# The opening of a decoder step in finer pieces, and raw weights held in four parts

## The chip, the cores and the metric

The kernel runs on one core of a Trainium2 chip. The metric is the device time of one execution in microseconds (us), the median of several runs. The engines have short names: PE is TensorE (matmuls; PEld its weight loads), DVE VectorE, ACT ScalarE, POOL GpSimd, SP SyncE, which issues most of the DMAs here.

## The reference

One layer of a hybrid decoder, for a prompt of 256 tokens and 8 single-token samples, which go through the projections together as 264 columns. All of it is float32.

```
proj = rms_norm(x, g_mix) @ w_in               # 2048 -> 1024+2*256+2048+3072+32
q, k, v, z, xbc, dt = split(proj)
x = x + concat(swa(q, k, v), ssd(z, xbc, dt)) @ w_out
x = x + cross_attend(rms_norm(x, g_cross), memory) @ w_co
x = x + (silu(gate) * val) @ w_down            # gate, val = conv(rms_norm(x, g_ffn) @ w_up)
```

`swa` is attention over a window of 128 with learned sinks, `ssd` a Mamba-2 mixer; the outputs hold the new caches and states too. Nearly all of the arithmetic is in the products with w_in, w_out, w_up and w_down.

## The kernel before

Activations stand with features on the 128 partitions and tokens along the columns. x is 16 blocks (`KB`) of 128 features by 264 tokens, in four tiles `xT[0..3]` of four blocks.

**Three products for one.** To multiply float32 numbers at the fast rate, each operand is split into a rounded part and a rest, both of type float32r: hi = round(x) on ScalarE (L87, L98), lo = x - hi on VectorE (L88, L99). `mm3` (L101) then issues three matmuls: hi.hi, hi.lo, lo.hi. For x the split also multiplies by the norm's gain, from the first 16 columns of `par`; the norm's own factor `r0` is applied when results leave PSUM.

**Weights** come as units of 2048 columns (1 MB): eight k-blocks of 256 output columns. `weights` (L69) takes a raw tile `wraw` of 2048 columns (two such buffers), loads it by one DMA on SP's queue, and makes two halves of 1024 columns, `whi` and `wlo` (four buffers each). A raw buffer is free again when both halves have been subtracted. `proj` runs the matmuls of two units for 256 output columns, and this goes on through the whole layer with other stages between: attention, the SSD scan, cross-attention and the convolutions. There is a priority for weights, and the order of instructions on the engines is set by the framework's planner, which simulates a timeline.

**The opening** (L149 to L191) is in a block in which SP, PE, ACT and DVE keep the order of the text. The memset of `acc0` feeds 14 warm-up matmuls (L156). SP issues `par`, the first quarter of x, the first unit of w_in in two pieces, the weights of dt (`w_dt`, 512 columns), three more quarters of x, and the second unit. `split_x(c)` splits four blocks. PE then runs, for the first 256 output columns, `first_k(k)` (six matmuls a block, into the two banks `first`) and for dt `dt_k(k)` (three a block, into `dt_ps`): 16 blocks each, so 96 and 48 matmuls. Behind the block come the squares of x (`sw`, L252 to L259) whose sum gives `r0`, which frees the banks of `first` and of dt.

ScalarE has to load a table before its first activation; before, that stands ahead of the first split of x.

Of the kernel before, what the change touches and what calls it, by code (L numbers as in the profile page):

```python
# [7 lines left out]
F32 = mybir.dt.float32  # L8
F32R = mybir.dt.float32r
AF = mybir.ActivationFunctionType  # L10
ALU = mybir.AluOpType
# [36 lines left out]
def hybrid_decoder_step_kernel(ctx: ExitStack, tc: tile.TileContext, I, O):  # L48
# [11 lines left out]
    def psum(tag):  # L60
        return ps.tile([128, 512], F32, tag=tag, name=tag, bufs=banks[tag])
# [7 lines left out]
    def weights(src, n=2048, into=None, step=2048):  # L69

        out = []
        with tc.high_priority():
            raw = wpool.tile([128, 2048], F32, tag="wraw", name="wraw", bufs=2)[:, :n]
            if step < n:
                for o in range(0, n, step):
                    nc.sync.dma_start(out=raw[:, o:o + step], in_=src[:, o:o + step])
            else:
                nc.sync.dma_start(out=raw, in_=src)
            for o in range(0, n, NPART):
                w = min(NPART, n - o)  # L80
                if into:
                    hi, lo = into
                else:
                    hi = wpool.tile([128, w], F32R, tag="whi", name="whi", bufs=WBUFS)
                    lo = wpool.tile([128, w], F32R, tag="wlo", name="wlo", bufs=WBUFS)
                x = raw[:, o:o + w]
                S.copy(out=hi, in_=x)  # L87
                V.tensor_tensor(out=lo, in0=x, in1=hi.bitcast(F32), op=ALU.subtract)  # L88
                out.append((hi, lo))
        return out  # L90
# [50 lines left out]
    def split_x(c):  # L141
        for k in range(4 * c, 4 * c + 4):
            split(A[k // 8][0][:, k % 8, :], A[k // 8][1][:, k % 8, :], xT[c][:, k % 4, :], par[:, k:k + 1])

    def load_x(c):
        nc.sync.dma_start(out=xT[c], in_=I["xT"][:, 4 * c:4 * c + 4, :])


    acc0 = small.tile([128, T], F32, tag="acc", bufs=1, name="acc0")  # L149
    dt_ps = psum("mm")  # L150
    first = [psum("t") for _ in range(2)]
    warm = psum("x")
    with tc.manual_schedule(engines={mybir.EngineType.SP, mybir.EngineType.PE, mybir.EngineType.Activation, mybir.EngineType.DVE}):
        V.memset(acc0, 0.0)
        for _ in range(14):
            PE.matmul(warm[:, :T], acc0[:, 0:128], acc0, start=True, stop=True)  # L156
        nc.sync.dma_start(out=par[:, 0:16], in_=I["par"][:, 0:16])
        load_x(0)
        split_x(0)
        pre = weights(w_in[0], step=1024)  # L160
        dthi, dtlo = (w.rearrange("p (k c) -> p k c", c=32) for w in weights(I["w_dt"], 512, (w2[:, 0:512], w2[:, 512:1024]))[0])
        for c in range(1, 4):
            load_x(c)
            split_x(c)
        pre = pre + weights(w_in[1])
# [4 lines left out]
        def first_k(k):  # L170
            wh, wl = (w.rearrange("p (k c) -> p k c", c=256) for w in pre[k // 4])
            for m in range(2):
                mm3(first[m][:, :T], wh[:, k % 4, m * 128:(m + 1) * 128], wl[:, k % 4, m * 128:(m + 1) * 128],
                    A[k // 8][0][:, k % 8, :], A[k // 8][1][:, k % 8, :], k == 0, k == KB - 1)
# [6 lines left out]
        for k in range(4):  # L181
            first_k(k)
        for k in range(4):
            dt_k(k)
        for k in range(4, 8):
            dt_k(k)
            first_k(k)
        for k in range(8, KB):
            dt_k(k)
        for k in range(8, KB):  # L190
            first_k(k)  # L191
# [61 lines left out]
    for i in range(2):  # L253
        for j in range(2):
            S.activation(out=sw[i][:, 4 * j:4 * j + 4, :], in_=xT[2 * i + j], func=AF.Square)
        V.tensor_tensor(out=sw[i][:, 0:4, :], in0=sw[i][:, 0:4, :], in1=sw[i][:, 4:8, :], op=ALU.add)
# [1034 lines left out]
```

## Time and profile before

| | |
|---|---|
| median of 3 runs | 1441.08 us (1439.83 to 1441.81) |
| the profiled execution | 1435.89 us, its span 1434.1 us |
| PE / DVE / ACT / POOL busy | 1413.7 / 1071.7 / 774.9 / 149.9 us |
| DMA | 304.64 MB, mean 212 GB/s over the span |
| granted clock, mean | 0.995 |

Times in the views count from the span's start. "xT<-in_xT_dram" is a write of the tile xT from the DRAM input xT; "<-" behind an idle time names what ended it; SPq is SP's queue of DMA issues. A row of the chain of waits has its start, its length and what ran or was waited for. Matmuls are pipelined: a row's own length is longer than the distance to the next start, and a stretch's count divided by its length gives the pace. "PEclk" or the number ahead of the DMA share is the granted clock of TensorE.

### The profile page before, as it was taken

How to read it: one execution, taken by the hardware profiler on the slowest of the kernel's cores; microseconds unless marked ns; L12 is line 12 of the kernel's file. 1: busy time of each engine (PE TensorE's matmuls, PEld its weight loads, DVE VectorE, ACT ScalarE, POOL GpSimd, SP SyncE). 2: the span in 40 equal slices, each digit the busy share in tenths (PEclk: the TensorE clock that was granted, in tenths of full speed). 3: DMA queues.
4: the chain of work that ended last, by engine and by line, in shares of the span. 5: the costliest groups of instructions: out<-in, count | busy, mean ns of one | idle time of the engine just before them, and what ended most of it. 6: DMA issues, size and time to landing. Idle time of an engine off the chain costs nothing.

```text
span 1434.1 us, 28668 instructions
## 1 busy us (share of the span) xinstructions
PE 1413.7 (99%) x11481; PEld 1387.9 (97%) x11481; DVE 1071.7 (75%) x2066; ACT 774.9 (54%) x1297; POOL 149.9 (10%) x330
## 2 busy tenths in 40 slices
PE   9999999999999999989999999999999999999999
PEld 8998899999999999978999999999999999999999
DVE  6849869999986777779677775677577757665664
ACT  6547754556645455656555653565355535543532
POOL 0000001111104212015001010001000100010000
PEclk9999999999999999999999999999999999999999
DMA  6853347776667556856566766566566655555554
GB/s 253 293 203 118 127 155 228 250 251 229 209 229 275 195 177 216 342 223 241 207 221 221 239 222 213 200 229 235 183 213 220 224 176 191 196 189 187 180 189 149
DMA packets 59365, 304.64 MB, mean 212 GB/s; under 512 B 8864, under 2 KB 13920, under 8 KB 29664
## 3 DMA queue, kind: packets, MB, share of 16 engines
q1 hardware_dynamic: 53728, 283.94, 56.5%
q0 software_dynamic: 5504, 18.88, 3.6%
q8 instruction: 90, 1.47, 0.4%
q14 instruction: 43, 0.35, 0.1%
HBM read 287.06 MB, written 16.28 MB: 212 GB/s over the span
## 4 chain that ended last, share of the span: by engine, by line
PE 89%; DVE 4%; DMA 4%; ACT 2%; POOL 1%; issue 1%; SPq 0%; ACTq 0%; DVEq 0%; POOLq 0%
PE mm L103 19%; PE mm L102 19%; PE mm L104 19%; PE t L102 9%; PE t L104 9%; PE t L103 9%; DVE wlo L88 1%; DMA wraw<-in_w_out_dram 1%; DMA vt<-in_mvT_dram 1%; ACT whi L87 1%; PE s L439 1%; DVE kt L924 1%; PE t L208 1%; DVE vt L953 1%; DMA wraw<-in_w_in_dram 1%
## 5 line engine op out<-in xcount | busy, mean ns | idle before, releaser
L87 ACT CAST whi<-wraw 128x1024 fp32r<-128x1024 f32 x448 | 466.1, 1049 | 531.7 <-PE mm L103 284.7
L88 DVE TENSOR_TENSOR wlo<-wraw,whi 128x1024 fp32r<-128x1024 f32 x448 | 552.4, 1238 | 229.4 <-ACT whi L87 227.6
L102 PE MATMUL t<-x2h,whi 128*128 128x264 f32 x704 | 200.7, 285 | 3.0 <-ACT whi L87 3.0
L103 PE MATMUL t<-x2l,whi 128*128 128x264 f32 x704 | 200.1, 284 | 0.0
L102 PE MATMUL mm<-x2h,whi 128*128 128x264 f32 x704 | 199.9, 284 | 0.2 <-DVE res L1023 0.2
L104 PE MATMUL t<-x2h,wlo 128*128 128x264 f32 x704 | 199.9, 284 | 0.0
L103 PE MATMUL mm<-x2l,whi 128*128 128x264 f32 x704 | 199.8, 284 | 0.0
L104 PE MATMUL mm<-x2h,wlo 128*128 128x264 f32 x704 | 199.4, 283 | 0.0
L103 PE MATMUL mm<-hl,whi 128*128 128x264 f32 x704 | 198.8, 283 | 0.0
L104 PE MATMUL mm<-hh,wlo 128*128 128x264 f32 x704 | 198.4, 283 | 0.0
L102 PE MATMUL mm<-hh,whi 128*128 128x264 f32 x704 | 197.5, 284 | 0.0
L102 PE MATMUL mm<-xh,whi 128*128 128x264 f32 x608 | 176.6, 292 | 0.7 <-ACT whi L87 0.7
L103 PE MATMUL mm<-xl,whi 128*128 128x264 f32 x608 | 175.0, 289 | 0.0
L104 PE MATMUL mm<-xh,wlo 128*128 128x264 f32 x608 | 174.6, 291 | 0.0
L102 PEld LDWEIGHTS t<-x2h,whi 128*128 128x128 f32 x704 | 133.1, 189 | 3.2 <-ACT whi L87 3.2
L103 PEld LDWEIGHTS t<-x2l,whi 128*128 128x128 f32 x704 | 133.2, 189 | 0.0
L102 PEld LDWEIGHTS mm<-x2h,whi 128*128 128x128 f32 x704 | 132.4, 188 | 0.4 <-ACT sq L220 0.4
L104 PEld LDWEIGHTS t<-x2h,wlo 128*128 128x128 f32 x704 | 132.4, 188 | 0.3 <-DVE wlo L88 0.3
L103 PEld LDWEIGHTS mm<-x2l,whi 128*128 128x128 f32 x704 | 132.6, 188 | 0.0
L103 PEld LDWEIGHTS mm<-hl,whi 128*128 128x128 f32 x704 | 132.5, 188 | 0.0
L104 PEld LDWEIGHTS mm<-x2h,wlo 128*128 128x128 f32 x704 | 132.1, 188 | 0.0
L104 PEld LDWEIGHTS mm<-hh,wlo 128*128 128x128 f32 x704 | 132.0, 188 | 0.0
(418 smaller groups left out, 3042.6 us busy)
## 6 DMA issues: line engine op xcount, KB each, us to landing
wraw<-in_w_up_dram SPq DMA_DIRECT2D x88, 1024.0 KB, 4.9
wraw<-in_w_in_dram SPq DMA_DIRECT2D x51, 1024.0 KB, 5.4
wraw<-in_w_dn_dram SPq DMA_DIRECT2D x44, 1024.0 KB, 4.9
wraw<-in_w_out_dram SPq DMA_DIRECT2D x24, 1024.0 KB, 4.9
h<-in_h_dram POOLq DMA_DIRECT2D x32, 256.0 KB, 5.0
hn<-in_h_dram SPq DMA_DIRECT2D x16, 512.0 KB, 6.7
out_state_s_dram<-hn POOLq DMA_DIRECT2D x16, 512.0 KB, 3.4
pb<-dram_p SPq DMA_DIRECT2D x4, 1028.0 KB, 10.0
```

Of the source, the lines that this page charges most:

```text
L87: S.copy(out=hi, in_=x)
L88: V.tensor_tensor(out=lo, in0=x, in1=hi.bitcast(F32), op=ALU.subtract)
L102: PE.matmul(out, wh, xh, start=start, stop=False)
L103: PE.matmul(out, wh, xl, start=False, stop=False)
L104: PE.matmul(out, wl, xh, start=False, stop=stop)
L208: PE.transpose(out, in_, cst[0:k, C_ID:C_ID + k])
L439: PE.matmul(s3, qT[:, j, c * 128:c * 128 + 128], kbd[:, pp, :, 0:nk], start=True, stop=True)
L924: V.scalar_tensor_tensor(out=x, in0=x, scalar=1.0, in1=qb[:, 2 * b + m, :], op0=ALU.mult, op1=ALU.mult, accum_out=lg[:, kb, row:row + 1])
L953: V.scalar_tensor_tensor(out=vt[:, b, m, :], in0=vt[:, b, m, :], scalar=1.0, in1=pbs[row // 8][:, row % 8, 0:256], op0=ALU.mult, op1=ALU.m ...
```

## The change

- The raw weights are held in four buffers of 1024 columns (`raw_part`), and every load is one of 1024 columns (512 KB, or 256 KB for dt) with its own buffer, in the whole kernel.
- ScalarE runs a Copy on one column (`table`) early, and issues two DMAs itself: par and the first 512 columns of the first unit.
- In the opening x is loaded in eight pieces of two blocks, the first unit in four pieces of 512 columns, in turn. The splits go block by block in the same turn; the first weight piece is rounded on VectorE.
- 8 warm-up matmuls instead of 14.
- `first_k` runs the three products of a block for both output halves in turn (hi.hi twice, hi.lo twice, lo.hi twice), and the order of blocks is: first 0 to 7, dt 0 to 7, first 8 to 15, dt 8 to 15.
- The squares of x are ordered behind the last split.

```diff
@@ -66,24 +66,22 @@
 
     NPART, WBUFS = 1024, 4
 
-    def weights(src, n=2048, into=None, step=2048):
+    def raw_part(n=NPART):
+        return wpool.tile([128, n], F32, tag="wraw", name="wraw", bufs=4)
+
+    def weights(src, n=2048, into=None):
 
         out = []
         with tc.high_priority():
-            raw = wpool.tile([128, 2048], F32, tag="wraw", name="wraw", bufs=2)[:, :n]
-            if step < n:
-                for o in range(0, n, step):
-                    nc.sync.dma_start(out=raw[:, o:o + step], in_=src[:, o:o + step])
-            else:
-                nc.sync.dma_start(out=raw, in_=src)
             for o in range(0, n, NPART):
                 w = min(NPART, n - o)
+                x = raw_part(w)
+                nc.sync.dma_start(out=x, in_=src[:, o:o + w])
                 if into:
                     hi, lo = into
                 else:
                     hi = wpool.tile([128, w], F32R, tag="whi", name="whi", bufs=WBUFS)
                     lo = wpool.tile([128, w], F32R, tag="wlo", name="wlo", bufs=WBUFS)
-                x = raw[:, o:o + w]
                 S.copy(out=hi, in_=x)
                 V.tensor_tensor(out=lo, in0=x, in1=hi.bitcast(F32), op=ALU.subtract)
                 out.append((hi, lo))
@@ -138,57 +136,109 @@
     for h in range(2):
         A.append((T3(apool, 8, F32R, "A", f"xh{h}", 4), T3(apool, 8, F32R, "A", f"xl{h}", 4)))
 
-    def split_x(c):
-        for k in range(4 * c, 4 * c + 4):
-            split(A[k // 8][0][:, k % 8, :], A[k // 8][1][:, k % 8, :], xT[c][:, k % 4, :], par[:, k:k + 1])
-
-    def load_x(c):
-        nc.sync.dma_start(out=xT[c], in_=I["xT"][:, 4 * c:4 * c + 4, :])
+    def load_x(j):
+
+        nc.sync.dma_start(out=xT[j // 2][:, 2 * (j % 2):2 * (j % 2) + 2, :], in_=I["xT"][:, 2 * j:2 * j + 2, :])
+
+    def x_of(k):
+        return xT[k // 4][:, k % 4, :], par[:, k:k + 1]
+
+    def x_hi(k):
+        x, g = x_of(k)
+        return S.activation(out=A[k // 8][0][:, k % 8, :], in_=x, func=AF.Copy, scale=g)
+
+    def x_lo(k):
+        x, g = x_of(k)
+        return V.scalar_tensor_tensor(out=A[k // 8][1][:, k % 8, :], in0=x, scalar=g, in1=A[k // 8][0][:, k % 8, :].bitcast(F32),
+                                      op0=ALU.mult, op1=ALU.subtract)
+
+
+    wraw0 = [raw_part() for _ in range(2)]
+    pre = [tuple(wpool.tile([128, NPART], F32R, tag=t, name=t, bufs=WBUFS) for t in ("whi", "wlo")) for _ in range(2)]
+
+    def w_piece(q):
+        cs = slice(512 * (q % 2), 512 * (q % 2) + 512)
+        return wraw0[q // 2][:, cs], pre[q // 2][0][:, cs], pre[q // 2][1][:, cs]
+
+    def w_load(q, on):
+        on.dma_start(out=w_piece(q)[0], in_=w_in[0][:, 512 * q:512 * q + 512])
+
+    def w_hi(q):
+        raw, hi, _ = w_piece(q)
+        S.copy(out=hi, in_=raw)
+
+    def w_lo(q):
+        raw, hi, lo = w_piece(q)
+        V.tensor_tensor(out=lo, in0=raw, in1=hi.bitcast(F32), op=ALU.subtract)
 
 
     acc0 = small.tile([128, T], F32, tag="acc", bufs=1, name="acc0")
+    table = small.tile([128, 1], F32, tag="r", bufs=2, name="table")
     dt_ps = psum("mm")
     first = [psum("t") for _ in range(2)]
     warm = psum("x")
     with tc.manual_schedule(engines={mybir.EngineType.SP, mybir.EngineType.PE, mybir.EngineType.Activation, mybir.EngineType.DVE}):
         V.memset(acc0, 0.0)
-        for _ in range(14):
+        load_x(0)
+        S.dma_start(out=par[:, 0:16], in_=I["par"][:, 0:16])
+        w_load(0, S)
+
+        S.activation(out=table, in_=acc0[:, 0:1], func=AF.Copy)
+        for _ in range(8):
             PE.matmul(warm[:, :T], acc0[:, 0:128], acc0, start=True, stop=True)
-        nc.sync.dma_start(out=par[:, 0:16], in_=I["par"][:, 0:16])
-        load_x(0)
-        split_x(0)
-        pre = weights(w_in[0], step=1024)
-        dthi, dtlo = (w.rearrange("p (k c) -> p k c", c=32) for w in weights(I["w_dt"], 512, (w2[:, 0:512], w2[:, 512:1024]))[0])
-        for c in range(1, 4):
-            load_x(c)
-            split_x(c)
-        pre = pre + weights(w_in[1])
+        for q in range(1, 4):
+            w_load(q, nc.sync)
+            load_x(q)
+        x_hi(0)
+        raw, hi, _ = w_piece(0)
+        V.tensor_copy(out=hi, in_=raw)
+        x_hi(1)
+        x_lo(0)
+        w_lo(0)
+        x_lo(1)
+        for q in range(1, 4):
+            w_hi(q)
+            w_lo(q)
+            for k in (2 * q, 2 * q + 1):
+                x_hi(k)
+                x_lo(k)
+        dthi, dtlo = (w.rearrange("p (k c) -> p k c", c=32) for w in weights(I["w_dt"].rearrange("p k c -> p (k c)"), 512, (w2[:, 0:512], w2[:, 512:1024]))[0])
+        for h in range(2):
+            raw = raw_part()
+            nc.sync.dma_start(out=raw, in_=w_in[1][:, 1024 * h:1024 * h + 1024])
+            hi, lo = (wpool.tile([128, NPART], F32R, tag=t, name=t, bufs=WBUFS) for t in ("whi", "wlo"))
+            for j in (4 + 2 * h, 5 + 2 * h):
+                load_x(j)
+            S.copy(out=hi, in_=raw)
+            V.tensor_tensor(out=lo, in0=raw, in1=hi.bitcast(F32), op=ALU.subtract)
+            pre.append((hi, lo))
+            for k in range(8 + 4 * h, 12 + 4 * h):
+                xsplit = x_hi(k), x_lo(k)
         nc.sync.dma_start(out=cst, in_=I["cst"])
         nc.sync.dma_start(out=par[:, 16:], in_=I["par"][:, 16:])
         nc.sync.dma_start(out=hcol, in_=I["hcol"])
 
         def first_k(k):
-            wh, wl = (w.rearrange("p (k c) -> p k c", c=256) for w in pre[k // 4])
-            for m in range(2):
-                mm3(first[m][:, :T], wh[:, k % 4, m * 128:(m + 1) * 128], wl[:, k % 4, m * 128:(m + 1) * 128],
-                    A[k // 8][0][:, k % 8, :], A[k // 8][1][:, k % 8, :], k == 0, k == KB - 1)
+            wh, wl = (w.rearrange("p (k c) -> p k c", c=256)[:, k % 4, :] for w in pre[k // 4])
+            xh, xl = (a[:, k % 8, :] for a in A[k // 8])
+
+            for i, (w, x) in enumerate(((wh, xh), (wh, xl), (wl, xh))):
+                for m in range(2):
+                    PE.matmul(first[m][:, :T], w[:, m * 128:(m + 1) * 128], x, start=k + i == 0, stop=k == KB - 1 and i == 2)
 
         def dt_k(k):
             mm3(dt_ps[0:32, :T], dthi[:, k, :], dtlo[:, k, :], A[k // 8][0][:, k % 8, :], A[k // 8][1][:, k % 8, :],
                 k == 0, k == KB - 1)
 
 
-        for k in range(4):
+        for k in range(8):
             first_k(k)
-        for k in range(4):
+        for k in range(8):
             dt_k(k)
-        for k in range(4, 8):
-            dt_k(k)
+        for k in range(8, KB):
             first_k(k)
         for k in range(8, KB):
             dt_k(k)
-        for k in range(8, KB):
-            first_k(k)
 
     def pc(name, i=0, n=1):
         o = _PC[name][0]
@@ -250,10 +300,11 @@
 
 
     sw = [T3(apool, 8, tag="B", name=f"sw{i}", bufs=4) for i in range(2)]
-    for i in range(2):
-        for j in range(2):
-            S.activation(out=sw[i][:, 4 * j:4 * j + 4, :], in_=xT[2 * i + j], func=AF.Square)
-        V.tensor_tensor(out=sw[i][:, 0:4, :], in0=sw[i][:, 0:4, :], in1=sw[i][:, 4:8, :], op=ALU.add)
+    with tc.issue_after(xsplit[0].ins), tc.issue_after(xsplit[1].ins):
+        for i in range(2):
+            for j in range(2):
+                S.activation(out=sw[i][:, 4 * j:4 * j + 4, :], in_=xT[2 * i + j], func=AF.Square)
+            V.tensor_tensor(out=sw[i][:, 0:4, :], in0=sw[i][:, 0:4, :], in1=sw[i][:, 4:8, :], op=ALU.add)
     V.tensor_tensor(out=sw[0][:, 0:4, :], in0=sw[0][:, 0:4, :], in1=sw[1][:, 0:4, :], op=ALU.add)
     V.tensor_tensor(out=sw[0][:, 0:2, :], in0=sw[0][:, 0:2, :], in1=sw[0][:, 2:4, :], op=ALU.add)
     V.tensor_tensor(out=acc0, in0=sw[0][:, 0, :], in1=sw[0][:, 1, :], op=ALU.add)
```

## The prediction

> **What bounds the kernel now.** I read the totals of the page first, then TensorE's list of waits, then the opening along the chain of waits and the timeline, then the chain round the longest later stall, and last the DMA and queue lists.
>
> The totals, and what TensorE waited for (microseconds in total, times, the longest):
>
> ```profile
> span 1434.1 us, 28668 instructions
> ...
> PE 1413.7 (99%) x11481; PEld 1387.9 (97%) x11481; DVE 1071.7 (75%) x2066; ACT 774.9 (54%) x1297; POOL 149.9 (10%) x330
> ...
> PE mm L102 <- ACT whi L87: 3.5, 2, 2.8
> ...
> PE y L853 <- ACT sq L898: 2.8, 1, 2.8
> PE t L104 <- DVE wlo L88: 1.6, 3, 0.7
> ```
>
> TensorE (PE) is the bound: 99% busy, VectorE 75%, ScalarE 54%. A change that leaves the matmuls alone can only win what PE loses: the time before its first useful matmul, and 20 us idle (1434.1 - 1413.7). The warm-up matmuls count as busy, so the opening's loss does not show in the 99%. It shows in the chain at the start (start, length, what):
>
> ```profile
> 0.74 0.39 SPq L157
> ...
> 1.19 3.98 DMA xT<-in_xT_dram
> ...
> 5.25 1.28 ACT L98
> ...
> 6.54 1.73 ACT xh L98 x4
> 8.27 0.97 ACT sw L255
> 9.25 0.94 ACT whi L87
> ...
> 10.21 1.24 DVE wlo L88
> ...
> 11.49 0.39 PE t L104
> ```
>
> x lands at 5.17. Only then does ScalarE load its table (1.28), split four blocks (1.73), take a sum-of-squares step that could wait (L255, about 1), and cast the first 1024 columns (0.94). On PE:
>
> ```profile
> 10.23 0.39 PE L102 MATMUL t<-xh,whi 128*128 128x264 f32 x1
> 10.46 0.28 PE L103 MATMUL t<-xl,whi 128*128 128x264 f32 x1
> 11.49 0.39 PE L104 MATMUL t<-xh,wlo 128*128 128x264 f32 x1 [0.75 <-DVE wlo L88]
> ```
>
> Useful work begins at 10.23 and runs on only from 11.49: 1.03 between two starts. Pace of PE in three stretches (length, busy and count, granted clock, DMA share, GB/s):
>
> ```profile
> 1.20:6.20 5.00, 5.00 (x11) 1.00 0.80 256
> 6.20:10.10 3.90, 3.90 (x18) 1.00 1.02 392
> 11.49:28.70 17.21, 17.21 (x141) 1.00 0.64 239
> ```
>
> From 11.49 to 28.70 there is a matmul every 0.122 us (17.21 / 141) and no gap: the opening's 144 matmuls (96 for the first columns, 48 for dt) are never starved again. So the opening's end is its start plus 17.6 us.
>
> **The change part by part.** *Warm-ups, 14 to 8.* Each is two instructions. Eleven of them fit into 1.20 to 6.20 (0.45 each), then 18 into 3.9 us (0.22 each). Sixteen are through at 6.2 + 5 x 0.22 = 7.3, and 7.4 with the step between the two paces. That is the earliest start of useful work.
>
> *The order of loads.* Before, SP issued par, then 528 KB of x, then weights. After, SP issues 264 KB of x first, and ScalarE's queue issues par (8 KB) and 256 KB of weights meanwhile. Data in the opening (length, PE, PEld, DVE, ACT, POOL busy; clock; DMA share; GB/s):
>
> ```profile
> 2.00:3.00 1.00, 1.00 (x4) 0.79 (x3) 0.00 (x0) 0.00 (x0) 0.00 (x0) 1.00 0.75 127
> 3.00:4.00 1.00, 1.00 (x3) 0.68 (x3) 0.00 (x0) 0.00 (x0) 0.00 (x0) 1.00 0.93 317
> 4.00:11.00 7.00, 6.75 (x25) 5.12 (x23) 2.50 (x5) 5.74 (x8) 0.00 (x0) 1.00 1.02 389
> ```
>
> About 450 KB have moved by 4.0, then 389 a us; the old par and x (536 KB) had moved by 4.2 and landed at 5.17, a lag of 1.0. The new x piece, par and weight piece together are 528 KB, and the first goes out at 0.74 instead of 1.19: moved by 4.2 - 0.45 and landed at about 4.7. Two DMA issues on ScalarE cost about 0.4 each by SP's row (0.39), beside the loads; the table's 1.28 follows and is over by about 3, also beside the loads. First useful operands: x split 0.43 (1.73 / 4), at the same time VectorE's cast of 512 columns, at most the 0.61 of ScalarE's cast below, hence 5.3. PE is not free before 7.4, so that cover is 2 us deep; if the first loads come over 2 us late, every further us costs one.
>
> *Feeding.* Costs of a half of 512 columns and of a block of x:
>
> ```profile
> 11.04 0.61 ACT L87 CAST w<-wraw 128x512 fp32r<-128x512 f32 x1
> ...
> 12.49 0.68 DVE L88 TENSOR_TENSOR w<-wraw,w 128x512 fp32r<-128x512 f32 x1
> ...
> 13.10 1.70 DVE L99 SCALAR_TENSOR_TENSOR xl<-xT,par,xh 128x264 fp32r<-128x264 f32 x4
> ```
>
> PE needs 12 x 0.122 = 1.46 us for two blocks; VectorE needs 0.68 + 2 x 0.43 = 1.54, ScalarE 0.61 + 0.86 = 1.47. VectorE's first pair (with its cast) ends at 4.7 + 0.6 + 1.54 = 6.8, the fourth at 6.8 + 3 x 1.54 = 11.4. The data for it: 2088 KB moved at 4.0 + (2088 - 450) / 389 - 0.45 = 7.8, landed 1.0 later by the lag above, plus one pair's 1.54: 10.3. PE reaches that pair at 7.4 + 3 x 1.46 = 11.8. So it is fed, by 0.4. SP's seven issues of x and weights end by 0.74 + 7 x 0.45 = 3.9. The last quarter of the second weight unit takes the first buffer again, free after 6.8 + 0.68 = 7.5, and five issues stand behind it on SP (two of x, cst, par, hcol). With dt, the unit's other half and the x between, its bytes have moved by 4.0 + (3896 - 450) / 389 - 0.45 = 12.4 and landed by 13.4; PE wants it at 7.4 + 96 x 0.122 = 19.1. The squares, which now stand behind the last splits, feed r0:
>
> ```profile
> 33.21 1.80 DVE L213 RECIPROCAL r<-r 128x264 f32<-128x264 f32 x1 [0.38 <-ACT r L212]
> ```
>
> It was there at 35.0 and wanted at 28.7 + 96 x 0.122 = 40.4, where the third pair of columns needs the dt bank: 5.4 to spare, and with the splits over earlier the squares start hardly later. All these I put at nothing, hidden by the slack named; without it each costs its lateness. The new order of the three products asks for the low weight last, which is what removes the 0.91 stall (1.03 less 0.12).
>
> *Opening's sum.* Start 10.23 to 7.4: 2.8. Stall 0.9. At most 3.7; I take 3.4, as VectorE is 0.08 slower than PE for each pair. Ends: nothing, were PE fed no faster than before, and 3.7.
>
> *Clock.* The row has the faster pace from 6.2, five us after the first warm-up. The Trainium skill (TensorE: Matmul & The Clock Gate, Part 1: The HAM clock gate) says that the array is released only by a busy window of about 3.4 us that runs freely, so the moment differs from run to run; the granted clock in these rows reads 1.00 throughout, and only the pace shows the step. By the trace's moment the opening gives 3.4; by that rule at its late end (8.0, an estimate from the page's window) it gives about 1 less.
>
> *Raw weights in quarters.* Every later load becomes two of 512 KB, each released by its own subtraction. It matters where PE waited for raw weights. The longest, in the chain round 404:
>
> ```profile
> 391.51 1.06 ACT whi L87
> ...
> 393.69 1.21 DVE wlo L88
> ...
> 394.93 7.92 DMA wraw<-in_w_out_dram
> ...
> 402.94 1.05 ACT whi L87
> ...
> 404.04 0.39 PE mm L102
> ```
>
> and the other half of the released buffer, on VectorE, with PE's count round it:
>
> ```profile
> 389.81 1.21 DVE L88 TENSOR_TENSOR wlo<-wraw,whi 128x1024 fp32r<-128x1024 f32 x1
> ...
> 400.00:404.00 4.00, 1.24 (x11) 1.00 0.85 305
> ```
>
> PE did 11 matmuls where 33 fit: about 2.8 lost (its wait row says 2.8). The first half was done with at 391.0, but the load waited for the second, to 394.93. After, it is issued 3.9 us earlier and carries half. What a half takes, issue to landing, is nearest to these:
>
> ```profile
> wraw<-in_w_up_dram SPq DMA_DIRECT2D x88, 1024.0 KB, 4.9
> ...
> res<-in_xT_dram SPq DMA_DIRECT2D x4, 528.0 KB, 3.9
> ...
> wraw<-in_w_in_dram SPq DMA_DIRECT2D x2, 512.0 KB, 5.7
> ```
>
> So 394.9 to 398.9 even at the crowded 7.92, cast by 400: no wait. I take 2.8 here, the rest (0.7 in the same row, 3.5 - 2.8, and smaller) at nothing since VectorE is late there too. Ends: a loss, priced as a rival, and 3.0 + 0.7 + 2.8 if that and the wait of L853 near 580 go too. Issues: 226 more at 0.33 to 0.4 on SP, which waits most of the time.
>
> *Against halves* speaks the Trainium skill (DMA: Bandwidth & Descriptors, Bandwidth): batch to 1 MiB for three quarters of the peak. Its fit (2.0 us plus bytes / 436 GB/s) gives 3.2 for a half and 4.4 for a whole (estimates from the page); the rows have 3.9 and 4.9, and pieces of 256 to 528 KB ran at 389 GB/s in the opening.
>
> **Sum.** 3.4 + 2.8 = 6.2. The profiled execution took 1435.89 for a span of 1434.1; it would be 1429.7. The median of the three runs is 1441.08, 5.2 above it, so the predicted median is 1434.9.
>
> **Rivals.** *Opening alone:* the rest is planned anew and the stall at 404 stays or moves. For it: VectorE, ScalarE and PE run in an order that follows from the program's plan. 1437.7.
>
> *The wait of L853 goes too.* The cast ahead of it on ScalarE waited for this load, issued behind a subtraction:
>
> ```profile
> 568.48 7.30 DMA wraw<-in_w_ck_dram
> ```
>
> 2.8 more: 1432.1. Against it: the landing of 7.30 shows a crowded queue, in which a half gains less.
>
> *The opening is fed no faster:* blocks arrive in the same FIFO, the start moves but PE then stalls, and only the 0.9 is left: 1440.2. Against it, the 389 GB/s.
>
> *The clock turns late:* sixteen instructions at 0.45 end at 8.4, 1.0 lost: 1435.9.
>
> *SP's waits (slower).* SP already waits for earlier landings before it issues weights:
>
> ```profile
> SPq L78 <- DVE wlo L88: 665.9, 132, 13.6
> SPq L78 <- DMA wraw<-in_w_in_dram: 28.7, 13, 5.1
> ...
> 583.90 12.74 DMA vt<-in_mvT_dram
> ```
>
> With twice the issues such waits come oftener, and a landing takes 12.74 near 584. A quarter held up behind one comes 12.74 - 4.9 = 7.8 late; from 3.4 on that eats the opening. 1441.1 + 7.8 - 3.4 = 1445.5. Against it: PE has up to four cast parts (11.7 us) in hand.
>
> *Halves do not overlap,* the page's rule taken to its end: 448 x 3.9 = 1747 us of loading, longer than the span: about 1750. The opening's 389 GB/s speaks against it.
>
> **How the numbers follow.** Forecast 0.34, opening alone 0.25, L853's wait too 0.10, fed no faster 0.13, clock late 0.05, SP's waits 0.08, no overlap 0.02, nothing at all 0.03. A measurement tells 0.2%, 2.9 us, from no change. Opening alone lies 0.5 past that line, so I count 0.19 of it as faster: 0.34 + 0.10 + 0.05 + 0.19 = 0.68 faster; 0.06 + 0.13 + 0.03 = 0.22 the same; 0.10 slower. The range runs from 1430.5 (L853's wait too, the 0.7, and what of the 1.6 of L104 is not the opening's 0.75) to 1440.5 (fed no faster); outside are 0.10 slower and some 0.05 below. The likeliest case alone, 1432 to 1437.
>
> **What would show it.** Right: a table load before 3 us; the first useful matmul at 7.4 to 8.4 and no gap over 0.3 behind it; the opening's last at about 25 instead of 28.7; no stall of 3 us near 400; a wraw landing near 3.9. Wrong: gaps on PE between 8 and 13 with x or weights as releaser; new rows of PE waiting for a cast that waited for a load; landings of a half near 5 in the steady stretches.

## The result, and the profile after

The changed kernel took **1425.38 us** (median of 4 runs, 1422.11 to 1426.13) against 1440.45 (1438.64 to 1441.81) for the kernel before on the same chip: a ratio of 0.9895, interval 0.9867 to 0.9924, or 15 us less. The forecast was 1434.9 with a range down to 1430.5: the sign was right, the size under half, and the time lies below the range.

The profiled execution took 1426.13, 9.8 less than the one of before (1435.89). The other 5 of the 15 lie in the executions: before's profiled one was among its quickest, after's the slowest of its four. The section on the prediction takes that up.

The totals of the page:

```profile
span 1424.3 us, 29300 instructions
...
PE 1408.7 (99%) x11469; PEld 1385.7 (97%) x11469; DVE 1067.6 (75%) x2069; ACT 774.4 (54%) x1299; POOL 142.7 (10%) x330
```

The longest rows of TensorE's list of waits (total, times, longest):

```profile
PE mm L100 <- DVE t L331: 1.9, 1, 1.9
PE y L275 <- POOL accx L271: 1.7, 1, 1.7
PE s L1049 <- ACT e L1021: 1.7, 1, 1.7
...
PE y L284 <- POOL accm L271: 1.0, 1, 1.0
```

Idle time fell only from 20.4 (1434.1 - 1413.7) to 15.6 (1424.3 - 1408.7), but busy time fell by 5 as well. Of these, 3.9 are the warm-ups, which count as busy: 9.0 of busy time stand ahead of the first useful matmul before, 5.1 after. A stretch at half clock counts as busy too, but this execution did not have less of that: between the opening's first matmuls and the end TensorE ran at half clock for 13.6 us before and for 17.1 after. The three long waits of before (2.8 to 3.0, two of them for a cast of weights, one at the attention's norm) have gone. New is the first row: the third pair of columns waits for `r0`.

**The opening.** On the timeline of the changed kernel, ScalarE's table load and then TensorE:

```profile
1.67 1.28 ACT L186 ACT_TABLE_LOAD   x1 [1.67 <-PEq L1326]
...
1.20 5.45 PE L188 MATMUL x<-acc 128*128 128x264 f32 x16 [1.20 <-DVE eps L254]
6.29 0.59 PE L227 MATMUL t<-xh,whi 128*128 128x264 f32 x2
...
36.25 0.28 PE L102 MATMUL mm<-xh,wlo 128*128 128x264 f32 x1
38.39 0.36 PE L100 MATMUL mm<-xh,whi 128*128 128x264 f32 x1 [1.86 <-DVE t L331]
```

Useful work starts at 6.29 and goes on without a gap of 0.3 to 36.25. Then 2.14 pass between two starts, with what follows it in the view by stretches (length, busy and count of PE, PEld, DVE, ACT, POOL; granted clock; DMA share; GB/s):

```profile
6.29:24.40 18.11, 18.11 (x147) 17.29 (x146) 16.12 (x33) 16.37 (x29) 0.00 (x0) 1.00 0.87 336
...
38.20:42.10 3.90, 3.71 (x18) 3.74 (x19) 3.24 (x9) 1.89 (x4) 0.00 (x0) 0.56 0.99 367
```

A granted clock of 0.56 is a stretch of 3.4 us at half clock with a little around it: 18 matmuls in 3.9 us where 32 fit, so 1.7 us lost behind a wait of 1.9.

**Where the time went.** The start of the matmul with the same number, counted from the last one, in both profiled executions (after less before; times are those of before; the order of the matmuls differs in places):

| stretch of before | after less before at its end | in the stretch | what |
|---|---|---|---|
| 0 to 36 | -4.7 | -4.7 | earlier start, no stall |
| 36 to 55 | -1.0 | +3.7 | wait for r0 (2.1), half clock (1.7) |
| 55 to 389 | -1.1 | -0.1 | 1.5 lost near 210 (a slow stretch of 6.8 for one of 3.4), won back by 389 |
| 389 to 410 | -4.3 | -3.3 | wait at 404 gone |
| 410 to 574 | -3.2 | +1.1 | new wait for the norm's sum (L284, 1.0) |
| 574 to 585 | -7.75 | -4.6 | wait of L853 gone, and its half-clock stretch |
| 585 to 675 | -5.5 | +2.2 | several small, a slow stretch of 6.8 from 622 for one of 3.4 |
| 675 to 686 | -10.4 | -4.9 | wait at 679 gone, and its half-clock stretch |
| 686 to the end | -10.4 | 0.0 | (the span ends 9.8 earlier) |

The three places by stretches, before and then after:

```profile
388.00:410.00 22.00, 19.20 (x153) 18.45 (x152) 20.32 (x40) 10.67 (x19) 1.33 (x1) 1.00 0.58 202
575.00:590.00 15.00, 12.24 (x92) 12.04 (x91) 12.82 (x72) 10.20 (x15) 0.00 (x0) 0.89 0.87 323
670.00:684.00 14.00, 11.01 (x78) 10.49 (x77) 10.70 (x14) 7.11 (x9) 2.94 (x5) 0.88 0.47 178
```

```profile
388.00:410.00 22.00, 22.00 (x180) 21.52 (x179) 20.47 (x42) 11.17 (x20) 3.34 (x2) 1.00 0.57 193
575.00:590.00 15.00, 15.00 (x128) 14.92 (x127) 12.66 (x63) 8.39 (x12) 0.00 (x0) 1.00 0.97 366
670.00:684.00 14.00, 14.00 (x118) 14.00 (x118) 11.39 (x18) 9.63 (x13) 0.68 (x5) 1.00 0.70 220
```

In the same 15 and 14 us TensorE does 36 and 40 matmuls more, and the granted clock goes from 0.89 and 0.88 to 1.00: wait and slow stretch went together there. The wait of 2.8 at 404 had no slow stretch behind it.

What held the third of them, on ScalarE's timeline before and after:

```profile
673.30 0.60 ACT L1096 ACTIVATE c<-u,par 128x256 f32<-128x256 f32 x1 [6.51 <-issue]
...
677.99 2.93 ACT L87 CAST whi<-wraw 128x1024 fp32r<-128x1024 f32 x3
```

```profile
665.08 1.05 ACT L85 CAST whi<-wraw 128x1024 fp32r<-128x1024 f32 x1 [2.00 <-DMA wraw<-in_w_up_dram]
667.82 0.60 ACT L1147 ACTIVATE c<-u,par 128x256 f32<-128x256 f32 x1 [1.70 <-DVE u L1134]
```

Before, the cast's load of 1 MB was issued at 663.44 and landed 10.8 later, at 674.2, and in ScalarE's order the cast stood behind two convolution steps (a chain through GpSimd and VectorE). After, the first quarter lands at 665 and its cast stands ahead of the convolution.

The loads themselves, a half now (KB, median us from issue to landing):

```profile
wraw<-in_w_up_dram SPq DMA_DIRECT2D x176, 512.0 KB, 3.9
wraw<-in_w_in_dram SPq DMA_DIRECT2D x102, 512.0 KB, 4.7
```

Twice as many; the half of w_up comes 1.0 sooner than the whole did (4.9).

### The profile page after: what moved, and what is told of

Same layout as the page of the kernel before. It is cut to its first block, busy times and chain, and to the rows that moved or that the text cites. A ratio compares the mean times of both kernels' runs of the same rounds, so it can differ in the third digit from the quotient of the medians.

```text
span 1424.3 us, 29300 instructions
## 1 busy us (share of the span) xinstructions
PE 1408.7 (99%) x11469; PEld 1385.7 (97%) x11469; DVE 1067.6 (75%) x2069; ACT 774.4 (54%) x1299; POOL 142.7 (10%) x330
## 4 chain that ended last, share of the span: by engine, by line
PE 91%; DVE 3%; DMA 2%; POOL 1%; ACT 1%; issue 1%; SPq 0%; ACTq 0%; POOLq 0%; DVEq 0%
PE mm L100 20%; PE mm L101 20%; PE mm L102 19%; PE t L100 9%; PE t L102 9%; PE t L101 9%; DVE wlo L86 1%; PE t L227 1%; DMA wraw<-in_w_out_dram 1%; PE s L490 1%; POOL accm L271 1%; DMA pb<-dram_p 1%; PE t L258 1%; PE t L519 1%; PE y L703 1%
## 5 line engine op out<-in xcount | busy, mean ns | idle before, releaser
L86 DVE TENSOR_TENSOR wlo<-wraw,whi 128x1024 fp32r<-128x1024 f32 x444 | 544.3, 1228 | 230.3 <-ACT whi L85 228.5
## 6 DMA issues: line engine op xcount, KB each, us to landing
pb<-dram_p SPq DMA_DIRECT2D x4, 1028.0 KB, 10.4
```

## The experiments

The theory: the gain comes from halves of a unit landing and being released by themselves, which removes long waits for weights with their half-clock stretches; the opening's own gain is mostly taken back by r0. The rivals: the opening carries the gain; the halves' size alone does it, not the ring of four; a new plan of the whole kernel removed the waits by chance.

Most edits make the planner write the order anew: with six warm-ups more, TensorE's order differs after 146 useful matmuls. So a single time within some 3 us says little of the edit; the waits in the trace say more. In three runs of parts 3 and 4 the order stayed: with the squares at high priority and with the square root's table the operations and tiles of all engines come in the order of the changed kernel, and without the early table they do but for six places on ScalarE and VectorE.

**1. The two parts alone** (one batch; before 1437.33 us).

The ring alone, in the kernel before:

```
-            raw = wpool.tile([128, 2048], F32, tag="wraw", name="wraw", bufs=2)[:, :n]
...
+                x = raw_part(w)          # [128, 1024], bufs=4
+                nc.sync.dma_start(out=x, in_=src[:, o:o + w])
```

> The kernel before with one edit: raw weights in four buffers of 1024 columns, one load each; its old opening stays. In the changed kernel the opening's gain of 4.6 us shrinks to 1.0 by 55 us, and 9.4 of the 10.4 come later. Theory Q (a quarter released by its own subtraction is loaded sooner, which removes the waits for raw weights near 404 and in front of L853 near 580): 6 to 10 us below before, and both waits gone. Theory P (every edit makes the planner put the work in another order, and the later waits move by chance): anywhere within 5 us of before, with other waits. Theory O (the opening carries the gain): within 1.5 us of before.

Measured: 1431.17 us, ratio 0.9948 (0.9929 to 0.9967). By the trace the waits near 404, 580 and 679 are gone, worth 3.3, 4.6 and 4.9; new waits (1.6 for the squares of q near 59, 1.6 for the scan near 297, 1.2 for the norm's sum near 460) and a slow stretch of 6.8 from 626 (3.4 before) take back nearly half (the span is 7.0 shorter).

The opening alone, with two raw buffers of 2048:

```
-    wraw0 = [raw_part() for _ in range(2)]
+    raw0 = wpool.tile([128, 2048], F32, tag="wraw", name="wraw", bufs=2)
+    wraw0 = [raw0[:, 0:1024], raw0[:, 1024:2048]]
```

> The changed kernel with raw weights as before: two buffers of 2048 columns, one load for a whole unit except in the opening. Theory Q: 1 to 4 us below before (the opening, less what a late r0 takes back), with the waits near 404 and in front of L853 still there. Theory P: anywhere within 5 us of before. Theory O: 10 to 15 us below before.

Measured: 1442.43 us, ratio 1.0034 (1.0015 to 1.0052): slower, where the theory had 1 to 4 us faster. Its useful work starts 4.1 earlier than before's, but then TensorE's timeline has three waits:

```profile
17.30 0.51 PE L231 MATMUL t<-xh,whi 128*128 128x264 f32 x2 [1.62 <-ACT xh L150]
18.54 0.51 PE L231 MATMUL t<-xl,whi 128*128 128x264 f32 x2 [0.74 <-DVE xl L154]
24.63 0.59 PE L102 MATMUL mm<-xh,whi 128*128 128x264 f32 x1 [3.17 <-ACT whi L87]
```

and SP's queue, of this kernel and then of the changed one, shows why:

```profile
4.21 0.53 SPq L78 DMA_DIRECT2D wraw<-in_w_dt_dram  x1
10.88 0.33 SPq L212 DMA_DIRECT2D wraw<-in_w_in_dram  x1
11.25 0.91 SPq L143 DMA_DIRECT2D xT<-in_xT_dram  x2
```

```profile
4.08 0.52 SPq L79 DMA_DIRECT2D wraw<-in_w_dt_dram  x1
5.17 0.33 SPq L208 DMA_DIRECT2D wraw<-in_w_in_dram  x1
5.54 1.27 SPq L141 DMA_DIRECT2D xT<-in_xT_dram  x2
```

With two whole buffers the second unit waits until 10.88 for a free one, and x stands behind it. With four parts it goes out at 5.17. So the opening needs the ring. The waits near 407, 583 and 682 are all there again (2.8, 1.9 and 1.8 between starts).

The two parts do not add up: the ring alone gives 6 us, the opening alone loses 5, and both together give 15. By the profiles the changed kernel's span is 2.8 below that of the ring alone (4.8 in the changed kernel's second profile, below). Of this the opening shows 0.9 (1.2) at 55, and the ring's wait near 59, which the changed kernel does not have, another 1.9. The rest, and why the medians show more (0.9948 against 0.9895), is open.

**2. Size or release.** The kernel before, every unit by two DMAs of 1024 columns into one buffer of 2048:

```
-    def weights(src, n=2048, into=None, step=2048):
+    def weights(src, n=2048, into=None, step=1024):
```

> The kernel before, where every unit is loaded by two DMAs of 1024 columns into one buffer of 2048 columns, so that the second load is sent with the first and the buffer is released whole. Theory Q: within 2 us of before, since the release is what counts, not the size of a transfer. A rival, smaller transfers land sooner and that suffices: 4 to 10 us below before. A second rival, more transfers are a burden: above before.

Measured: 1433.58 us, ratio 0.9967 (0.9953 to 0.9981). Near 404 TensorE is fully busy, and of the wait at 679 only starts 0.5 and 0.8 apart are left (3.6 of the 4.9 us are gained):

```profile
388.00:410.00 22.00, 22.00 (x179) 21.52 (x178) 22.00 (x39) 11.22 (x20) 2.45 (x2) 1.00 0.71 229
575.00:590.00 15.00, 12.45 (x90) 11.84 (x89) 11.23 (x65) 9.07 (x14) 0.00 (x0) 0.90 0.96 329
```

but near 586 L853 still waits 1.8, with a half-clock stretch. Smaller transfers alone, with the buffer still released whole, remove most of two of the three, which the theory did not expect (it had this kernel within 2 us of before); the interval overlaps that of the ring, so what the release by parts adds isn't told apart in the total.

The changed kernel with three raw parts instead of four:

```
-        return wpool.tile([128, n], F32, tag="wraw", name="wraw", bufs=4)
+        return wpool.tile([128, n], F32, tag="wraw", name="wraw", bufs=3)
```

> The changed kernel with three raw parts of 1024 columns instead of four. If what the quarters bring is that a load is issued as soon as one part is free, with the parts of two units under way at once, then one part less brings back about the old waits: one of 2 to 3 us near 404 and one or two more of the three at 404, 580 and 679, with the half-clock stretches behind them: 1429 to 1434 us. Rival: a load of half the size is enough by itself, three parts still hold one being cast and two under way: 1423 to 1427 with no wait of over 2.5 us at those three places. Rival: already the opening starves, since the second unit's loads wait for the first unit's casts: a gap before 20, over 1434.

Measured: 1429.96 us, ratio 0.9933 (0.9913 to 0.9953), about 5 above the changed kernel. The time was the one the ring theory gave, the place was not: near 404 two starts lie 0.7 apart, near 587 two, near 679 none. What came is the wait for r0, twice as long, with two half-clock stretches behind it (6.8 us from 40.0):

```profile
41.12 0.56 PE L100 MATMUL mm<-xh,whi 128*128 128x264 f32 x1 [4.13 <-DVE t L331]
```

```profile
388.00:410.00 22.00, 21.55 (x173) 20.84 (x172) 21.64 (x42) 12.68 (x20) 3.27 (x2) 1.00 0.65 209
575.00:590.00 15.00, 14.46 (x120) 14.01 (x120) 12.15 (x75) 9.49 (x15) 0.00 (x0) 1.00 0.98 344
670.00:684.00 14.00, 14.00 (x117) 14.00 (x117) 11.30 (x17) 8.64 (x12) 1.00 (x6) 1.00 0.64 206
```

So three parts are enough at the later places; the fourth counts in the start-up. That halves and not chance remove the later waits is made likely by a count: in the two kernels with whole units (before, and the opening alone) all three are there; in the twelve others, all with halves, no gap between starts at 404 and 679 is over 0.8, and L853's wait is left at over 0.5 in one. These twelve have eight different orders of TensorE, much alike in the later stages, so they are not twelve independent draws. With the ring of four and the new opening, some executions have a shorter one near 585 for another cause (1.0 to 2.2, behind L975).

**3. The wait for r0.** The changed kernel again, in the second batch (before 1440.28):

> The changed kernel itself, beside the three that follow and on their chip. By its first runs 12 to 18 us below before. Its execution should again show the bank wait near 38 and some windows of 3.4 us at half clock; if the spread of the times is made of such windows, the time falls by about 1.7 us for each window fewer, that is by 1.2 to 1.7 us for 0.001 more granted clock.

Measured: 1424.13 us, ratio 0.99 (0.9879 to 0.9921). In this execution the clock turned late (warm-ups until 7.58), the wait for r0 was 2.11, and no half-clock stretch followed it, nor was there one anywhere behind the start. At 55 it stands 1.3 ahead of before. So the wait is as long with a start 1.3 later, as r0 came 1.1 later too (38.9); the half clock behind it is a matter of the execution. A wait of 1.9 near 585 (L975), which the first execution does not have, stands here in the same order of work. The four times do not follow the granted clock as expected: 1424.18 at a mean clock of 1.000, 1423.69 at 0.995.

The squares and sums at high priority:

```
+    with tc.high_priority():
+        with tc.issue_after(xsplit[0].ins), tc.issue_after(xsplit[1].ins):
```

> The changed kernel with the squares of x, their sums and r0 at the priority of the weights. In the changed kernel TensorE waits 2.0 us at 36.4 for the bank that r0 frees, and a window of 3.4 us at half clock follows, 1.7 more. If that wait is what gives the opening's gain back: 3 to 4 us below the changed kernel, about 1422, and no wait there. If the weights' casts are then late instead: no better, or up to 3 us worse.

Measured: 1423.59 us, ratio 0.9902 (0.988 to 0.9923). The order did not change on any engine and the wait (1.9) stood as before: nothing learned on r0, but one more set of runs of the changed kernel's order.

The table that the early activation loads, changed to that of the square root which r0 needs:

```
-        S.activation(out=table, in_=acc0[:, 0:1], func=AF.Copy)
+        S.activation(out=table, in_=acc0[:, 0:1], func=AF.Sqrt)
```

> The changed kernel, whose early one-column activation is a square root instead of a copy, so that the table for r0's root is loaded at the start and not at 34. Theory R (the wait for r0 near 38 is what takes the opening's gain back): r0 comes 1.3 earlier, the wait of 2.0 shrinks to 0.7, and if that is too short for the clock to drop, 1.7 more: 1.3 to 3 us below the changed kernel. Rival, another wait takes its place (the evacuation on VectorE, or a table loaded again elsewhere): no difference.

Measured: 1425.82 us, ratio 0.9906 (0.9886 to 0.9926). A failure: the table is loaded a second time all the same, and r0 comes 3 us later, so that the wait grows to 4.1:

```profile
36.07 1.05 ACT L85 CAST whi<-wraw 128x1024 fp32r<-128x1024 f32 x1 [3.16 <-DMA wraw<-in_w_in_dram]
37.13 1.28 ACT L262 ACT_TABLE_LOAD   x1
```

The cast ahead of this load waits for weights. Another load of a table, of 1.28, stands at 21.67, where the changed kernel has none (L426 needs an exponential). As the order of the work is that of the changed kernel, this is a run in which r0 moves and the plan does not: TensorE comes to the wait as far ahead of before as in the repeat (4.0 and 3.8 at 36), and at 55 it is 3.0 behind before, where the changed kernel is 1.0 ahead. So the time of r0 sets the length of the wait, and the half clock behind it (6.8 here) adds to it.

The dt results in another PSUM bank, so that the third pair of columns needs no r0:

```
-    dt_ps = psum("mm")
+    dt_ps = psum("s")
```

> The changed kernel with the dt product in the bank that attention uses later, so that a third bank is free for the third pair of columns. Theory R in another way: TensorE has 12 matmuls (1.5 us) more before it needs r0, the wait falls from 2.0 to about 1: 1 to 3 us below the changed kernel. Rival: the planner, given another bank, moves the work behind it; then 3 us either way.

Measured: 1423.7 us, ratio 0.9892 (0.987 to 0.9914). The wait for r0 is gone; another of nearly its size stands 13 us on:

```profile
51.53 0.39 PE L102 MATMUL mm<-xh,wlo 128*128 128x264 f32 x1 [1.57 <-DVE wlo L86]
```

Both edits at once:

> The two edits together, the square root's table at the start and the dt product in another bank. Theory R: no wait for r0 at all and no window at half clock near 38, 3.7 us below the changed kernel, the best of all so far. Rival, the wait was cover for something else that is late: no better than either alone.

Measured: 1426.18 us, ratio 0.9911 (0.9892 to 0.993): no better, with waits of 2.2 and 2.6 between starts near 52 and 340.

Third batch (before 1438.69). Squares and sums in the hand-made order of ScalarE and VectorE:

```
-    with tc.issue_after(xsplit[0].ins), tc.issue_after(xsplit[1].ins):
+    with tc.manual_schedule(engines={mybir.EngineType.Activation, mybir.EngineType.DVE}):
```

> The changed kernel with the squares and the five adds behind them written into the hand-made order of ScalarE and VectorE, so that at most three of the casts' subtractions stand between the adds instead of five. If r0 is late because those subtractions go first on VectorE, r0 comes about 2 us earlier, TensorE's wait of 2.1 us near 38 goes, and with it the 3.4 us at half clock behind it (1.7): 1420 to 1422 us. Rival: the rest is planned anew and a wait of the same size comes up elsewhere, as with the dt bank moved: 1423 to 1426. Rival: the subtractions that now stand behind the adds are late themselves and TensorE waits for them near 26: over 1426.

Measured: 1423.79 us, ratio 0.9888 (0.987 to 0.9907). The wait is gone and TensorE is busy right through 30 to 60:

```profile
30.00:60.00 30.00, 30.00 (x246) 29.80 (x245) 25.65 (x42) 18.80 (x27) 0.00 (x0) 1.00 0.76 270
```

But this doesn't show why: `r0` came only 0.8 earlier (37.0), and TensorE arrived 2.3 later: it started 0.5 later and had short waits in the opening, of which the longest, 0.7 for dt's weights at 15.0, stands behind the first add on VectorE. At 55 it is 2.5 ahead of before. The total is as the rival had it: a wait of 2.4 comes up at 334 in the new plan.

So the adds themselves were taken away: a further kernel leaves out the last three adds of the sum (its `r0` is that of one block), with the opening untouched. Before took 1441.22 in its batch.

```
-    V.tensor_tensor(out=sw[0][:, 0:4, :], in0=sw[0][:, 0:4, :], in1=sw[1][:, 0:4, :], op=ALU.add)
-    V.tensor_tensor(out=sw[0][:, 0:2, :], in0=sw[0][:, 0:2, :], in1=sw[0][:, 2:4, :], op=ALU.add)
-    V.tensor_tensor(out=acc0, in0=sw[0][:, 0, :], in1=sw[0][:, 1, :], op=ALU.add)
-    r0 = total(acc0, D, "r0")
+    r0 = total(sw[1][:, 0, :], D, "r0")
```

> The changed kernel without the last three adds of the sum of squares (4 + 2 + 1 blocks; 2.3 us on VectorE): r0 is taken from one block of squares alone, all other work is the same. If r0 is late because these adds stand between the subtractions of weights on VectorE, r0's sum is there by about 23 instead of 30.5, r0 by 32 to 35 instead of 37.8, TensorE comes to its third pair of columns at 36 as before the wait and goes on without one: at 55 it is 3 to 4.5 us ahead of the kernel before instead of 1.0; in time 1420 to 1423 us, unless the new plan puts waits elsewhere. Rival: r0's chain follows TensorE's own order and ScalarE's casts: r0 still comes after 37 and the wait of 2 us stays: 1424 to 1426.

Measured: `r0` is there at 29.2, TensorE starts at 6.31 as in the changed kernel and has no wait at its third pair of columns:

```profile
24.02 3.47 DVE L86 TENSOR_TENSOR wlo<-wraw,whi 128x1024 fp32r<-128x1024 f32 x3
27.42 1.78 DVE L263 RECIPROCAL r<-r 128x264 f32<-128x264 f32 x1
```

It is 4.4 ahead of before at 36 and still at 55, where a wait of 1.0 for the squares of q takes 1.2. So with an `r0` that comes early the wait is gone, and the forecast's opening holds until 55. Which part of the chain to `r0` made it late this run does not tell, as leaving out 2.3 us of adds moved the whole chain, by 8.6; the section on the prediction looks at that. The time, 1423.97 (ratio 0.9893, 0.9864 to 0.9922), does not show the 3 us that the profile does (span 1418.7): its five runs spread from 1420.4 to 1427.2.

**4. The opening's other two parts.** 14 warm-ups instead of 8:

```
-        for _ in range(8):
+        for _ in range(14):
```

> The changed kernel with 14 warm-up matmuls instead of 8. They end at about 9.1 us instead of 6.3 (by the after profile: seven at 0.45 from 1.2 on, the other 21 instructions at 0.22). If the opening's start is set by the warm-ups, the first useful matmul comes 2.8 later; by 36 the delay is still there, and the wait of 2.1 for r0 swallows what of r0's chain does not follow TensorE. Between 0.6 and 2.8 slower than the changed kernel: 1424.7 to 1427 us. Rival: the wait for r0 swallows all of it: 1424, no difference. Rival: the clock's moment moves as well, so that the start is less than 1.5 later.

Measured: 1423.62 us, ratio 0.9886 (0.9868 to 0.9905).

```profile
1.20 8.62 PE L188 MATMUL x<-acc 128*128 128x264 f32 x28 [1.20 <-DVE eps L254]
9.47 0.60 PE L227 MATMUL t<-xh,whi 128*128 128x264 f32 x2
```

Useful work starts at 9.47, 3.2 later, and the time is the same, as the rival had it, though not for its reason. Its plan has no wait for r0 (TensorE is busy through 30 to 60), and at 55 it is 1.8 ahead of before: the changed kernel was 1.0.

Without the early table:

```
-        S.activation(out=table, in_=acc0[:, 0:1], func=AF.Copy)
```

> The changed kernel without the early activation that makes ScalarE load its table beside the loads: the table is loaded at the first split instead, for 1.28 us from about 3.7 on. If the warm-ups (until 6.3) cover it, the first useful matmul stays at 6.3 and no gap over 0.3 us follows: within 0.5 us of the changed kernel, 1423.5 to 1425 us. Rival: ScalarE's casts and splits are a chain at TensorE's own pace, so that the 1.28 comes back as gaps between 6 and 13: 1425 to 1426, with those gaps in the trace.

Measured: 1423.7 us, ratio 0.9886 (0.9866 to 0.9905). The load stands in front of the first split, and no gap follows:

```profile
4.21 1.28 ACT L148 ACT_TABLE_LOAD   x1 [4.21 <-DMA xT<-in_xT_dram]
...
6.85 0.60 PE L226 MATMUL t<-xh,whi 128*128 128x264 f32 x2
```

The warm-ups end at 6.8 in this execution and cover it. The early table is worth nothing that can be measured here.

No version beats the changed kernel by more than the intervals.

## Why the prediction was wrong

The mechanism was right in the main: loads in halves remove waits for weights (what the release by halves adds to the smaller loads is not told apart). The step that failed is where this was let count: "the rest (0.7 in the same row, 3.5 - 2.8, and smaller) at nothing since VectorE is late there too". Two more long waits went, the one of L853, which was kept as a rival at 0.10, and the one at 679. They were worth 4.6 and 4.9, against 3.3 for the one in the sum, and that put the time below the range. In the profiles the forecast -6.2 became -10.4: -1.0 for the opening (by 55), -3.3, -4.6 and -4.9 for the three waits, and some 3.3 given back elsewhere.

*The opening: right at first, wrong in the end.* Forecast -3.4; by 36 it was -4.7. The start came 1.1 earlier than the 7.4, as the clock turned at 4.5 in this execution and not at 6.2; that is the chance of the execution, and the repeat gave 7.58. The table lies beside the loads, the 0.91 stall is gone, and the pieces arrive in time, all as said. Then 3.7 are given back.

*The step that failed there: "All these I put at nothing, hidden by the slack named", of r0 with "5.4 to spare".* r0 was taken to come at 35.0 still, and TensorE to want it at 40.4. But 40.4 was reckoned from 28.7, the end of the opening before. With the prediction's own end, "about 25", it is 25 + 96 x 0.122 = 36.7, so only 1.7 were to spare. TensorE came at 36.4, and r0 was ready only at 37.8. VectorE's timeline before and after, with TensorE's product of the sum after, shows where the chain was later:

```profile
21.81 1.25 DVE L257 TENSOR_TENSOR sw<-sw,sw 128x1056 f32<-128x1056 f32 x1
...
27.57 0.41 DVE L259 TENSOR_TENSOR acc<-sw 128x264 f32<-128x264 f32 x1
```

```profile
23.76 1.24 DVE L308 TENSOR_TENSOR sw<-sw,sw 128x1056 f32<-128x1056 f32 x1
24.93 2.34 DVE L86 TENSOR_TENSOR wlo<-wraw,whi 128x1024 fp32r<-128x1024 f32 x2
27.20 0.69 DVE L309 TENSOR_TENSOR sw<-sw 128x528 f32<-128x528 f32 x1
27.82 2.34 DVE L86 TENSOR_TENSOR wlo<-wraw,whi 128x1024 fp32r<-128x1024 f32 x2
30.09 0.41 DVE L310 TENSOR_TENSOR acc<-sw 128x264 f32<-128x264 f32 x1
...
35.99 1.80 DVE L263 RECIPROCAL r<-r 128x264 f32<-128x264 f32 x1 [0.57 <-ACT r L262]
```

```profile
33.63 0.61 PE L275 MATMUL y<-acc,cst 128*128 128x264 f32 x2
```

The sum is ready at 30.5 (28.0 before). Of these 2.5, 2.0 are there at the first of the three adds (23.76 against 21.81): the squares now all stand behind the last splits, and ScalarE ends them at 21.3 instead of 19.5, where the prediction had "the squares start hardly later". The two subtractions of weights ahead of each of the last two adds account for little of the difference: from the first add to the sum it takes 6.7, and 6.2 before. From the sum to r0 it is 7.3 (7.0 before): TensorE multiplies the sum only at 33.63 in its order, and ScalarE loads its table at 34.18, behind a cast of weights that had itself waited 1.8 for TensorE. So the consumer was moved by 4 us and the slack was reckoned with its old time, while the producer came 2.8 later. That r0's time makes the wait is shown: with the order unchanged, the square root's table made r0 later and the wait longer, and without the three adds r0 came early and the wait was gone. How much of the chain the planner would move with an earlier sum is not shown.

*The wait at 404: right.* Forecast 2.8, measured 3.3 with what lay around it; 3.3 also with the ring alone.

*The wait of L853: a rival at 0.10 and 2.8; it was 4.6.* The argument against it, that in a crowded queue a half gains less, did not hold: the median landing of w_ck went from 6.1 for a whole to 4.4 for a half. And the price lacked the half-clock stretch behind the wait.

*The wait at 679: the largest single term, and not in the sum.* The sentence on the rest looked only at the row of 3.5; the row beside it in before's list, of nearly the same size, was not read:

```profile
PE t L102 <- ACT whi L87: 3.0, 1, 3.0
```

That is the same kind of wait, for a cast of weights on ScalarE and not for VectorE, and was worth 4.9.

*The clock* was weighed for the start alone. Before's profile has four half-clock stretches of 3.4 us behind the start (from 207.8, 579.9, 631.1 and 678.9), two of them behind waits that the change removes: 1.7 each that the idle time does not show. The changed kernel's first profile has three, of 3.4, 6.8 and 6.8 (from 38.6, 205.9 and 622.3), so it lost more to the clock in all, its second profile none.

*The offset.* The sum was made against a profiled execution and 5.2 added for the median. In the third batch the mean granted clock of the kernel before was 0.993 in the median of its runs, of the changed kernel's four runs 0.994 to 0.998. What is missing from a mean of 1 is the time lost (a stretch of 3.4 at half clock lacks 1.7), so an estimate of the loss is 0.007 x 1438 = 10 us before and 0.0045 x 1425 = 6 after (the middle of its four). So the medians hold about 4 us of clock. The two profiled executions stand the other way: at 0.995 and 0.994 the same estimate gives a loss of 7 before and 8.5 after. Together that is about the 5 us between the 9.8 of the profiles and the 15 of the medians. The means are rounded to 0.001, some 1.4 us, so this is rough; and that fewer long waits are what raised the clock is likely but not shown.

*Rivals:* SP's extra waits did not show as waits on TensorE; halves overlap (366 GB/s between 575 and 590). The Trainium skill (DMA: Bandwidth & Descriptors, Bandwidth) advises batches of 1 MiB; here two loads of 512 KB for each unit were faster than one of 1 MB (0.9967, 0.9953 to 0.9981). The waits near 404 and 679 ended with the cast of a first half, which can start before the second half lands. That halves do not overlap at all was the prediction's own extension of that advice; the page does not state it.

What stays open: how much of the rest is the planner's chance. Waits of 1 to 2.4 come and go between plans (near 59, 334, 456) and one near 585 between executions of the same plan, and no run held the plan fixed while the loads were changed. The nine kernels with the ring of four and the new opening have medians between 1423.6 and 1426.2.

## What to carry to other kernels

When a tuned kernel's bound engine is 99% busy, list every wait of over 2 us on it, and ask of each whether the change touches its cause: the change in buffers, meant for one place, was worth most at the two I had set aside. When a stage is made earlier, recheck the slack of everything it consumes with the new time at which it will be wanted, and with the producer's chain written out, not with the old times of either. Before crediting an earlier start, look at the next join behind it: here 4.7 us were in hand at 36 and 1.0 at 55.

## What the runs showed of the hardware

A wait of TensorE of only 1.9 us can be followed by 3.4 us at half clock; each such stretch costs 1.7 us and counts as busy. It need not follow: behind the wait of 2.8 at 404 before and the one of 2.1 in the changed kernel's second profile none followed. Nor does it take a wait: the stretch from 207.8 before follows 32 matmuls of 8 columns, 3.6 us long, with no idle time. The same kernel has from none (one execution of the changed kernel) to several, and its time mostly moves with the mean granted clock (24 runs of the kernel before: 1444.5 us at 0.989, 1431.9 at 0.996). The Trainium skill (TensorE: Matmul & The Clock Gate, Part 1: The HAM clock gate) gives a free-running window of about 3.4 us, and the stretches' length agrees; it puts the slow state after at least one idle window of about 3.4 us, and here the idle time before was 1.9, 2.8 and 3.0, so the measurement differs from it. The moment at which the clock first turned lay between 4.2 and 7.1 us in these executions, which in the changed kernel moves the end of its 16 warm-up instructions from 6.3 to 7.6.
